# Another order for a hand-scheduled conv and max-pool kernel: weight blocks copied ahead of the casts, one more block turned before the first product

## The chip, the cores and the metric

The kernel runs on one core of one Trainium2 chip. The metric is the device time of one execution in microseconds (us), lower is better; runs are compared by their median. Engines are named as in the profile: PE is TensorE, DVE is VectorE, ACT is ScalarE, POOL is GpSimd, SP is SyncE, which issues DMAs.

## The reference

The input `x` is 16 images of 64 channels and 64 x 64 pixels, `weight` is 128 filters of 64 x 3 x 3, all float32. The reference is a 3 x 3 convolution with zero padding of one pixel, followed by a 2 x 2 maximum:

```python
conv[b, co] += weight[co, ci, kh, kw] * x_pad[b, ci, kh:kh+h, kw:kw+w]
...
output[b, c, i, j] = np.max(conv[b, c, 2*i:2*i+2, 2*j:2*j+2])
```

The output is 16 x 128 x 32 x 32 in float32.

## The kernel before, in words

**Tiling.** Two images lie on the 128 partitions, 64 channels each; a pair p of images has its own bf16 tile `xb[p]` of 66 rows (a zero row above and below). A step s takes 16 rows of a pair (one of four quarters, `PLACES`), which give eight output rows for each of the two images, h = 0 and 1. There are 32 steps; the last is cut into two halves, 31 and 32. Each image's product uses only 64 rows of PE's array, so the two images run side by side: PE works in two lanes, and `product` (L252) issues a matmul of one lane, then one of the other. One product is three matmuls (the three columns of the filter, L206) of up to 512 columns, into one of the eight PSUM banks.

**The computation.** A pooled row is the maximum of two convolution rows that share input rows, so the kernel works with differences and sums of input rows and of filter rows. For steps of kind W (`TYPES`, L37) it forms e (`row_e`), s (`row_sum`) and d (`row_d`) from `xb`, with `combine` (L300): a joint one covers two neighbouring quarters in one instruction of 1024 columns, a single one 512. Products P2 and P0 go to a bank ta, P3 and P1 to a bank tb; `seed` (SE) copies ta to tb, `evac` (EV) copies ta to SBUF, `rowmax` (MX) takes the maximum into tb on DVE, P1 adds the s product, `odd` (OD) copies the odd columns out on ACT, `colmax` (CM) takes the maximum with the even ones on DVE and sends the output when both images are done. With `+`, OD copies nothing and CM reduces directly. Steps of kind K use the rows of `xb` themselves: PA1, PA2 into ta, PB1, PB2 into tb, and PR adds the s product. Step 0 runs in half pieces, F.k.part: F.0 and F.1 go to ta, F.2 and F.3 to tb (`first_product`, L267).

**The weights.** The filter arrives as `wraw` in float32 (DMA at L81). g0, g1 and g2 are its three filter rows, cast to bf16 blocks of `wq` (`raw_block`, L166). D2 is g2 - g1, D0 is g0 - g1, GS is g0 + g2, GM and GP are GS - g1 and GS + g1 (L412 to L415). PE turns a block by three or four 128 x 128 transposes into a PSUM bank (TG0, TD2 and so on: `turn`, L142), and DVE or ACT copies it to `wt` (VG0, VD2 and so on: `turn_out`, L152). The ring blocks G1, GM and GP need one column block copied first (uG1, uGM, uGP: `ring`, L128), on ACT with a `+`, else on POOL. F.0 needs VD2, F.1 VG0, F.2 VD0 and F.3 VG2; PR and PRA need VG1, P2 needs VGM, P1 needs VGP. Eight matmuls on constants (L506) stand ahead of all turns.

**The rows.** Of pair 0, 49 rows come in float32 by SP's queue: `kfirst` in two pieces (L95), `ksecond` (L97) and `kthird` (L99). They are cast to `xb[0]` by XOa, XEa (odd and even rows of the first piece of kfirst), XOb, XEb (second piece), X1, X2 (ksecond), X3 and X4 (kthird). F.0 and F.1 read the XO rows, F.2 and F.3 the XE rows. The last 15 rows of pair 0 (L.0.49.64) and all other pairs (L.p.lo.hi, `load`, L327) come by POOL's queue, which casts on the way.

**What sets the order.** Nothing is scheduled by a tool: `ORDER` (L444) is a list of tokens written out, and each engine gets its instructions in that order. `BANKS` (L498) gives, in order of need, the PSUM bank of each turn, ta and tb. An engine waits for the data and for its bank to be free. POOL's instructions and loads also wait for the DVE operation on rows or weights that stands last ahead of them in the list (`on_gpsimd`, L70), and the first load waits for D2. A `+` moves a token to its other engine: EV, SE, D on DVE instead of ACT or POOL; E on POOL instead of DVE; XO, XE on ACT instead of DVE; `&` makes S and E joint. The V copies go to ACT for G0, G2 and GM and to DVE for D2, D0, G1 and GP, and a `+` exchanges that (L155); a g is cast on ACT, or on DVE with a `+`.

Closing access: for s = 32 `colmax` reads the two banks ta and tb of the image in one instruction,

```python
in_=acc[:, a : b + 1 : b - a, i0:i1].rearrange("p k r (w two) -> p r w k two", two=2)
```

Of the kernel before, what the change touches and what calls it, by code (L numbers as in the profile page):

```python
# [11 lines left out]
def kernel(  # L12
# [424 lines left out]
    for m in ("G0", "G1", "G2"):  # L437
# [17 lines left out]
        PB1.5.1 S.10 P3.6.1 P2.7.0 PA2.9.0 CM.2.1 MX.6.0 MX.6.1 P1.6.0 PB2.5.1 P2.7.1 D.10 OD.4.0 SE.7.0
        EV.9.0 MX.5.1 OD.6.0 P1.6.1 P0.7.0 P3.7.0 PR.5.1 P2.8.1 SE.7.1 EV.7.0 CM.4.0 CM.6.0 OD+.6.1 D.8 P2.8.0
        P0.7.1 CM.6.1 P3.7.1 PB1.9.0 MX.7.0 OD.5.1 CM.5.1 P1.7.0 SE.8.0 SE.8.1 E&.10 S.11 D+.11 P0.8.1 EV.7.1
        PB2.9.0 E&+.12 P0.8.0 OD.7.0 P3.8.0 EV.8.1 P2.10.1 P2.2.0 MX.7.1 EV.8.0 L.5.0.64 MX.9.0 PR.9.0 P3.8.1
        CM.7.0 MX.8.0 P1.8.0 P1.7.1 SE.10.1 P0.10.1 OD.7.1 P3.10.1 SE.2.0 P0.2.0 EV.10.1 MX.8.1 P2.11.0 CM.7.1
        P3.2.0 S&.12 P1.8.1 P2.10.0 MX.10.1 OD.8.0 OD.9.0 PA1.9.1 P1.10.1 CM.8.0 CM.9.0 D.14 PA1.15.1 OD.8.1  # L460
        EV.2.0 CM.8.1 SE.11.0 OD.10.1 SE.10.0 MX.2.0 PA2.9.1 P0.11.0 P1.2.0 CM.10.1 P0.10.0 P3.10.0 PB1.9.1
        P3.11.0 EV.11.0 PA1.15.0 EV.9.1 OD.2.0 P2.12.1 EV.10.0 D+.12 SE.12.1 S&.14 PA2.15.1 PB2.9.1 D+.13
        S&.17 MX.10.0 CM.2.0 MX.11.0 MX.9.1 D.19 L.6.0.64 P1.10.0 P0.12.1 PA2.15.0 EV.15.1 P2.11.1 P3.12.1
        EV.12.1 E+.14 OD.10.0 CM.10.0 SE.11.1 P1.11.0 EV.15.0 PR.9.1 P2.12.0 OD.11.0 P0.11.1 MX.12.1 CM.11.0
        P1.12.1 P2.13.0 OD.9.1 CM.9.1 D+.16 E&.20 S&.18 SE.12.0 EV.11.1 P0.12.0 E&.18 P2.14.1 P3.12.0 E&+.16
        SE.13.0 EV.12.0 P0.13.0 P3.11.1 SE.14.1 OD.12.1 D.17 P2.13.1 EV.13.0 SE.13.1 CM.12.1 P0.14.1 P3.13.0
        MX.12.0 P3.14.1 EV.14.1 MX.13.0 P2.14.0 P0.13.1 MX.11.1 SE.14.0 P1.12.0 P3.13.1 OD.12.0 P1.13.0
        MX.14.1 P0.14.0 P1.11.1 EV.13.1 P1.14.1 D.18 PB1.15.0 OD.13.0 CM.12.0 MX.13.1 CM.13.0 OD.11.1 PB1.15.1
        P3.14.0 D.21 PB2.15.0 P2.16.0 P2.17.1 CM.11.1 EV.14.0 OD.14.1 SE.17.1 CM.14.1 MX.14.0 MX.15.0 P1.14.0
        PR.15.0 P1.13.1 OD+.13.1 PB2.15.1 CM.13.1 SE.16.0 MX.15.1 P2.19.0 OD.14.0 P0.17.1 OD+.15.0 P3.17.1  # L470
        CM.15.0 PR.15.1 EV.17.1 MX.17.1 P0.16.0 P2.18.1 SE.19.0 CM.14.0 P3.16.0 OD.15.1 EV.16.0 P0.19.0
        P1.17.1 S&.21 MX.16.0 CM.15.1 P2.16.1 SE.18.1 OD.17.1 EV.19.0 P3.19.0 CM.17.1 MX.19.0 P0.18.1 SE.16.1
        P1.16.0 OD+.16.0 P2.18.0 P1.19.0 P3.18.1 EV.18.1 P2.17.0 P0.16.1 P3.16.1 SE.18.0 MX.18.1 EV.16.1
        OD.19.0 D.20 L.7.0.64 E&.22 P1.18.1 P2.21.1 P0.18.0 SE.17.0 CM.16.0 MX.16.1 OD.18.1 EV.18.0 P3.18.0
# [85 lines left out]
```

## Time and profile before

| what | us |
|---|---|
| median of 3 runs (103.0 to 103.2) | 103.07 |
| the profiled execution | 103.78 |
| its span, first to last instruction | 102.0 |
| PE busy | 95.7 |
| DVE busy | 91.2 |
| ACT busy | 82.3 |
| POOL busy | 56.7 |

The profile is of one execution. "Span" runs from the first to the last instruction of the program; the execution's own time is 1.78 us longer. A row of the timeline gives start, duration, engine, line of the kernel, operation, what is written and read, shape and count, and in brackets the idle time of the engine before it and what ended it. A row of the windows gives the stretch, its length, then for PE, PEld (PE's weight loads), DVE, ACT and POOL the busy time and the number of instructions, then the granted clock of PE, the share of the DMA engines and GB/s. The durations of matmuls overlap, so their starts are what to read.

### The profile page before, as it was taken

The numbers are of one execution on the slowest core, as the hardware profiler recorded it, in microseconds if no ns is written. First come the engines' busy times: TensorE is split into PE (matmuls) and PEld (weight loads), VectorE is DVE, ScalarE is ACT, GpSimd is POOL, SyncE is SP. The second block draws the span as 40 slices with busy tenths as digits, with TensorE's granted clock in tenths as the row PEclk, the third lists the DMA queues.
The fourth block names the chain that finished last, engine by engine and source line by source line (L and its number), as shares of the span: only waits on it lengthen the run. The fifth ranks groups of instructions, "written<-read, shape, count | busy, mean of one in ns | idle before, by whom it ended". The sixth has DMA issues, their size and how long they took to land.

```text
span 102.0 us, 2471 instructions
## 1 busy us (share of the span) xinstructions
PE 95.7 (94%) x897; PEld 59.5 (58%) x897; DVE 91.2 (89%) x199; ACT 82.3 (81%) x182; POOL 56.7 (56%) x43
## 2 busy tenths in 40 slices
...
GB/s 75 263 322 175 162 171 214 225 235 231 228 218 245 327 202 191 240 209 212 143 330 151 116 146 190 202 284 105 70 231 14 16 195 107 103 103 0 135 202 86
DMA packets 11293, 18.04 MB, mean 177 GB/s; under 512 B 784, under 2 KB 9360, under 8 KB 10640
## 3 DMA queue, kind: packets, MB, share of 16 engines
...
q10 hardware_dynamic: 272, 0.13, 0.4%
q8 instruction: 7, 0.11, 0.4%
...
## 4 chain that ended last, share of the span: by engine, by line
PE 88%; DMA 5%; DVE 1%; ACT 1%; SPq 0%; issue 0%; DVEq 0%
PE acc L197 88%; DMA kfirst<-in_x_dram 5%; DVE o L378 1%; PE acc L146 1%; ACT wt L162 0%; ACT xb L401 0%; SPq L81 0%; DVEq L555 0%
## 5 line engine op out<-in xcount | busy, mean ns | idle before, releaser
L197 PEld LDWEIGHTS <-wt 64*128 64x128 bf16 x864 | 56.2, 94 | 33.1 <-issue 4.2
L197 PE MATMUL acc<-d,wt 64*128 64x504 bf16 (+3 forms) x312 | 63.4, 373 | 0.0
L322 POOL TENSOR_TENSOR d<-xb 128x1024 bf16<-128x1024 bf16 x18 | 38.1, 2129 | 17.1 <-DVE s L308 9.0
L197 PE MATMUL acc<-s,wt 64*128 64x504 bf16 (+3 forms) x204 | 47.2, 367 | 0.0
L360 DVE TENSOR_TENSOR acc<-acc,ev 128x512 f32<-128x512 f32 (+1 forms) x64 | 42.1, 683 | 1.8 <-ACT od L370 0.4
L197 PE MATMUL acc<-e,wt 64*128 64x512 bf16 (+2 forms) x156 | 38.2, 372 | 0.0
L355 ACT COPY acc<-acc 128x512 f32<-128x512 f32 (+1 forms) x52 | 29.6, 576 | 3.5 <-PE acc L197 2.3
L349 ACT ACTIVATE ev<-acc 128x512 f32<-128x512 f32 (+1 forms) x51 | 29.9, 595 | 2.0 <-PE acc L197 1.3
L197 PE MATMUL acc<-xb,wt 64*128 64x504 bf16 (+6 forms) x192 | 27.2, 333 | 0.5 <-ACT wt L162 0.5
L370 ACT COPY od<-acc 128x256 f32<-128x256 f32 (+1 forms) x51 | 18.6, 374 | 5.2 <-PE acc L197 3.1
L389 DVE TENSOR_TENSOR o<-acc,od 128x256 f32<-128x256 f32 (+1 forms) x51 | 20.2, 410 | 0.9 <-ACT od L370 0.6
L308 POOL TENSOR_TENSOR e<-xb 128x512 bf16<-128x512 bf16 (+1 forms) x8 | 12.2, 1523 | 5.3 <-PE acc L197 2.7
L328 POOL DMA_DIRECT2D xb<-in_x_dram x11 | 6.2, 564 | 10.5 <-DVE xb L403 6.7
L308 DVE TENSOR_TENSOR s<-xb 128x1024 bf16<-128x1024 bf16 (+1 forms) x20 | 11.4, 575 | 0.2 <-ACT xb L401 0.2
L385 DVE TENSOR_REDUCE o<-acc 128x256 f32<-128x512 f32 x13 | 8.9, 682 | 0.2 <-PE acc L197 0.2
L345 ACT COPY ev<-acc 128x512 f32<-128x512 f32 x11 | 6.4, 588 | 0.9 <-PE acc L197 0.6
L308 DVE TENSOR_TENSOR e<-xb 128x1024 bf16<-128x1024 bf16 (+1 forms) x8 | 5.2, 649 | 0.0
L322 DVE TENSOR_TENSOR d<-xb 128x1024 bf16<-128x1024 bf16 (+1 forms) x8 | 5.2, 647 | 0.0
L506 PE MATMUL acc<-const-bfloat16-1.0 128*128 128x512 bf16 x8 | 3.6, 628 | 0.8 <-PEq L541 0.8
L146 PEld LDWEIGHTS <-wq 128*128 128x128 bf16 x25 | 2.2, 132 | 1.7 <-issue 0.8
L146 PE MATMUL acc<-ident,wq 128*128 128x128 bf16 x25 | 2.9, 291 | 0.0
L506 PEld LDWEIGHTS <-const-bfloat16-1.0 128*128 128x128 bf16 x8 | 1.0, 139 | 2.4 <-issue 2.4
(29 smaller groups left out, 18.0 us busy)
## 6 DMA issues: line engine op xcount, KB each, us to landing
...
xb<-in_x_dram POOLq DMA_DIRECT2D x5, 1024.0 KB, 11.4
...
xb<-in_x_dram POOLq DMA_DIRECT2D x1, 528.0 KB, 11.1
ksecond<-in_x_dram SPq DMA_DIRECT2D x1, 512.0 KB, 6.4
kthird<-in_x_dram SPq DMA_DIRECT2D x1, 512.0 KB, 7.1
...
```

What stands on the lines that cost most here:

```text
L146: nc.tensor.transpose(tp[:, (j - lo) * CO : (j - lo + 1) * CO], wq[:, j : j + 2, :].rearrange("a b c -> a (b c)"), ident,)
L197: nc.tensor.matmul(acc[:, t, i0:i1, o0:o1], wt[lo : lo + CI, tap_of(m0, kw, h), :], rows(lo, i0, i1, c0, c1), start=start and kw == 1, sto ...
L308: note(engine.tensor_tensor(out=dst, in0=in0, in1=in1, op=op))
L322: engine.tensor_tensor(out=row["d", s][:, 0:n, :], in0=t[:, f + 1 : f + 1 + n, :], in1=t[:, f - 1 : f - 1 + n, :], op=SUB)
L328: inst = on_gpsimd(nc.gpsimd.dma_start(out=xb[p][:, lo + 1 : hi + 1, :], in_=rows_of(p, lo, hi)))
L345: (nc.vector.tensor_copy if alt else nc.scalar.copy)(out=dst, in_=src)
L349: nc.scalar.mul(dst, src, -1.0)
L355: (nc.vector.tensor_copy if alt else nc.scalar.copy)(out=acc[:, t, i0:i1], in_=acc[:, ta[s, h], i0:i1])
L360: nc.vector.tensor_tensor(out=t, in0=t, in1=ev[s][:, h, i0:i1], op=MAX)
L370: nc.scalar.copy(out=dst, in_=acc[:, tb[s, h], i0:i1, 1::2])
L385: nc.vector.tensor_reduce(out=o[:, h, i0:i1], in_=t.rearrange("p r (w two) -> p r w two", two=2), axis=mybir.AxisListType.X, op=MAX)
L389: nc.vector.tensor_tensor(out=o[:, h, i0:i1], in0=t[:, :, 0::2], in1=od[s][:, h, i0:i1], op=MAX)
```

## The change

Only `ORDER` and `BANKS` differ; no function is touched. The tokens of the products are the same ones, in another order.

- Up to the first product, F.0.0, the old list turns five blocks (G2, D2, G1, D0, G0: 19 transposes), the new one six (D2, G0, D0, G1, G2, GP: 22). GM is turned later in both. The change was described in a few words as two more blocks turned ahead of the first product; by the list it is one, GP.
- Casts of the weights: D2 is first on DVE, g2 moves from DVE to ACT, GP comes fourth on DVE, and uGP moves from ACT to POOL.
- Copies out: VG0 moves from DVE to ACT, ahead of XOa; VD2 from ACT to DVE; VG2 from ACT to DVE; VGP from ACT to DVE. XEa moves from DVE to ACT, so that all four casts of kfirst are there, XOa, XEa, XOb, XEb, with uGM before the last.
- Loads: L.0.49.64 is the first on POOL's queue instead of the third; L.1.0.17 follows GM instead of XEa.
- Row operations: d on DVE eleven times instead of eight; e on DVE joint three times and single twice instead of seven and one, on POOL joint six times and single six times instead of three and five; s joint 15 times and single twice instead of 12 and 8; OD with `+` twelve times instead of thirteen.
- The end: the last pair of products is P1.31.0 with PRB.32.1 instead of PA2.32.0 with P1.31.1, and CM.31.1, CM.32.0, CM.32.1, CM.31.0 close, where it was CM.32.1, CM.32.0, CM.31.1.

The diff, cut to its beginning, two lines of the middle and its end:

```diff
     ORDER = """
-        g2+ g1 D2 g0 TG2 TD2 uG1+ XOa+ TG1 VD2+ VG2 D0 XOb+ GS+ XEa XEb+ X2 TD0 L.1.0.17 TG0 VD0 L.1.17.33
-        VG0+ F.0.0 GP uGP+ F.2.0 F.0.1 F.3.1 GM F.1.0 S.0 X1+ F.1.1 EV+.0.1 EV.0.0 F.3.0 F.2.1 VG1+ uGM+
-        PA1.1.0 PB1.1.0 L.0.49.64 PA2.1.0 MX.0.1 MX.0.0 PB2.1.0 PA1.1.1 PB1.1.1 PR.0.0 X4 PR.0.1 X3 L.1.33.64
-        L.2.0.33 S.1 L.2.33.64 OD+.0.1 PA2.1.1 CM.0.1 EV.1.0 PB2.1.1 S.3 PB1.3.1 PA1.3.0 PB1.3.0 MX.1.0
-        PA1.3.1 EV.1.1 OD.0.0 L.3.0.64 PA2.3.0 TGM MX.1.1 PR.1.1 PR.1.0 CM.0.0 PB2.3.1 PA2.3.1 S.2 OD.1.1
-        PB2.3.0 D+.2 E&.2 CM.1.1 VGM EV.3.0 OD+.1.0 TGP P2.4.1 PA1.5.0 CM.1.0 MX.3.0 PA1.5.1 PB1.5.0 EV.3.1
-        PA2.5.1 PA2.5.0 PR.3.0 SE.4.1 MX.3.1 D.4 VGP+ P0.4.1 PB2.5.0 P2.2.1 S.4 P3.4.1 EV.5.0 P2.4.0 PR.3.1
-        S.5 E&.6 S&.7 EV.5.1 EV.4.1 OD.3.0 P2.6.0 SE.2.1 MX.5.0 L.4.0.64 CM.3.0 PR.5.0 SE.4.0 P0.2.1 P3.2.1
-        OD.3.1 P0.4.0 P3.4.0 MX.4.1 EV.2.1 D.6 OD+.5.0 EV.4.0 CM.3.1 P2.6.1 PA1.9.0 SE.6.0 SE.6.1 CM.5.0 E+.8
...
-        P0.29.1 P2.31.0 P3.29.1 CM.28.1 SE.30.0 EV.30.1 EV.29.1 P0.30.0 D+.31 S&.30 P3.30.0 P2.31.1 MX.28.0
-        EV.30.0 SE.31.0 MX.30.1 MX.29.1 P1.28.0 P1.30.1 MX.30.0 P0.31.0 SE.31.1 OD.28.0 P0.31.1 P3.31.1
-        CM.28.0 P3.31.0 P1.29.1 EV.31.0 P1.30.0 MX.31.0 PB1.32.0 PA1.32.1 EV.31.1 OD.30.1 CM.30.1 PB1.32.1
-        P1.31.0 PRA.32.1 PA1.32.0 PB2.32.0 OD.30.0 PRB.32.0 MX.31.1 OD.31.0 OD.29.1 PRB.32.1 CM.30.0 PB2.32.1
-        CM.31.0 PA2.32.1 PRA.32.0 CM.29.1 P1.31.1 PA2.32.0 CM.32.1 CM.32.0 OD.31.1 CM.31.1
+        D2 g0 TD2 g2 GS+ D0 GP g1 TG0 uG1+ VG0 VD2 TD0 TG1 TG2 XOa+ uGP L.0.49.64 VD0 TGP XEa+ XOb+ VG2+ GM
+        uGM+ F.0.0 XEb+ F.2.0 L.1.0.17 F.1.0 L.1.17.33 F.0.1 F.1.1 F.2.1 X2 EV.0.1 X1+ L.1.33.64 EV+.0.0 F.3.0
+        F.3.1 X3 X4 PA1.1.1 PB1.1.1 MX.0.0 VGP PA2.1.1 S.0 PB2.1.1 PA1.1.0 PB1.1.0 PA2.1.0 PA1.3.1 PB1.3.1 S.1
+        L.2.0.33 PB2.1.0 VG1+ L.2.33.64 MX.0.1 EV.1.0 EV.1.1 MX.1.0 PR.0.0 PA1.3.0 PA2.3.1 OD.0.0 S&.5 PR.1.0
+        OD.1.0 PA2.3.0 CM.0.0 TGM PB2.3.1 MX.1.1 PR.1.1 PA1.5.0 PB1.3.0 EV.3.1 PA2.5.0 VGM PB1.5.0 PR.0.1
+        PA1.5.1 EV.3.0 OD.1.1 L.3.0.64 CM.1.0 E+.2 MX.3.1 D+.2 PB2.3.0 PR.3.1 OD.0.1 EV.5.0 PB2.5.0 PA2.5.1
+        S&.4 OD.3.1 P2.2.1 E.4 CM.1.1 EV.5.1 CM.0.1 SE.2.1 CM.3.1 MX.3.0 P2.4.0 PR.3.0 P2.4.1 P0.2.1 MX.5.0
+        D.4 S&.7 E&.6 D+.6 SE.4.1 P0.4.1 PR.5.0 SE.4.0 OD.3.0 CM.3.0 OD.5.0 P3.4.1 E+.8 EV.4.1 L.4.0.64 P3.4.0
+        P3.2.1 CM.5.0 P2.6.1 EV.2.1 P0.4.0 MX.4.1 EV.4.0 P1.4.1 P2.6.0 SE.6.0 PA1.9.0 SE.6.1 MX.2.1 P1.2.1
+        P0.6.0 D+.7 OD.4.1 OD.2.1 PA2.9.0 EV.6.0 S&.11 D+.10 CM.2.1 D.8 P3.6.0 L.5.0.64 MX.4.0 P2.7.0 P0.6.1
+        P3.6.1 EV.6.1 EV.9.0 P1.4.0 MX.6.0 P1.6.0 PB1.5.1 SE.7.0 PB2.5.1 OD.4.0 MX.6.1 P2.8.1 P1.6.1 CM.4.1
+        MX.5.1 OD.6.0 PR.5.1 P3.7.0 SE.8.1 P0.8.1 P0.7.0 P2.7.1 OD.6.1 CM.4.0 CM.6.0 P2.8.0 CM.6.1 EV.7.0
...
+        P2.21.1 OD+.18.1 SE.21.1 CM.18.1 MX.18.0 D+.22 P1.16.1 P3.17.0 P1.18.0 EV.17.0 OD.16.1 P2.22.0 P2.19.1
+        P3.19.1 SE.22.0 EV.19.1 SE.20.0 D.20 P1.21.1 P0.22.0 OD+.17.0 CM.17.0 D.23 MX.19.1 P2.22.1 P3.22.0
...
+        SE.29.1 P0.30.0 OD.28.1 P3.30.0 EV.30.0 MX.28.0 P1.28.0 P2.31.0 P0.29.1 CM.28.1 MX.30.0 SE.31.1
+        P1.30.0 P3.29.1 EV.29.1 OD+.28.0 MX.29.1 P0.31.1 SE.31.0 P0.31.0 P1.30.1 P3.31.0 CM.28.0 EV.31.1
+        PB1.32.0 OD.30.0 CM.30.0 OD.30.1 PA1.32.0 PRB.32.0 P3.31.1 P1.29.1 MX.31.1 PA1.32.1 EV.31.0 PRA.32.0
+        PB1.32.1 P1.31.1 OD.29.1 CM.30.1 PB2.32.0 PB2.32.1 CM.29.1 OD.31.1 MX.31.0 PA2.32.0 PRA.32.1 PA2.32.1
+        CM.31.1 CM.32.0 P1.31.0 PRB.32.1 CM.32.1 OD.31.0 CM.31.0
     """
     BANKS = (
-        "0123456710346520137365417346027351426507431270652347105234651370451275302641057631256401723451670312"
-        "745632071634025674123706153427601526314"
+        "0123456701246753240546307124156371053246713041507632140362051376042375106245273165473026145076342561"
+        "047531205634072514675012643572041574325"
     )
```

More of the change, by code (lines that the diff above doesn't have):

```diff
@@ L455 @@
[L455 to L474, printed above, removed]
@@ new lines @@
+        P3.2.1 CM.5.0 P2.6.1 EV.2.1 P0.4.0 MX.4.1 EV.4.0 P1.4.1 P2.6.0 SE.6.0 PA1.9.0 SE.6.1 MX.2.1 P1.2.1
+        P0.6.0 D+.7 OD.4.1 OD.2.1 PA2.9.0 EV.6.0 S&.11 D+.10 CM.2.1 D.8 P3.6.0 L.5.0.64 MX.4.0 P2.7.0 P0.6.1
+        P3.6.1 EV.6.1 EV.9.0 P1.4.0 MX.6.0 P1.6.0 PB1.5.1 SE.7.0 PB2.5.1 OD.4.0 MX.6.1 P2.8.1 P1.6.1 CM.4.1
+        MX.5.1 OD.6.0 PR.5.1 P3.7.0 SE.8.1 P0.8.1 P0.7.0 P2.7.1 OD.6.1 CM.4.0 CM.6.0 P2.8.0 CM.6.1 EV.7.0
+        SE.8.0 E&+.11 P3.8.1 PB1.9.0 EV.8.1 OD+.5.1 SE.7.1 CM.5.1 S&.12 S&.8 P0.8.0 P2.10.1 PB2.9.0 MX.7.0
@@ new lines @@
+        P3.8.0 P0.7.1 MX.9.0 EV.8.0 P1.7.0 PR.9.0 SE.10.1 EV.7.1 P3.7.1 P0.10.1 D.11 OD.7.0 MX.8.0 MX.7.1
+        CM.7.0 EV.10.1 P3.10.1 P2.2.0 D.14 MX.8.1 MX.10.1 SE.2.0 OD.9.0 P1.7.1 P1.8.0 P2.11.0 CM.9.0 P1.8.1
+        OD.8.0 OD.7.1 OD.8.1 P1.10.1 P0.2.0 SE.11.0 P3.2.0 CM.8.0 E&+.12 CM.7.1 CM.8.1 EV.2.0 OD+.10.1 CM.10.1
+        PA1.9.1 PA1.15.1 MX.2.0 PB1.9.1 PA2.15.1 PA2.9.1 P0.11.0 EV.11.0 P2.10.0 P1.2.0 SE.10.0 EV.15.1 D+.12
+        PB2.9.1 PA1.15.0 EV.9.1 P0.10.0 OD.2.0 E.16 P2.11.1 PA2.15.0 S&.15 S&.19 D+.16 MX.9.1 EV.10.0 P2.12.1
```

45 lines of the change are left out of this document (27 added, 18 removed).

## The prediction

> **What bounds the kernel now.** I read the page first: the busy shares, then its chain of work.
>
> ```profile
> span 102.0 us, 2471 instructions
> PE 95.7 (94%) x897; PEld 59.5 (58%) x897; DVE 91.2 (89%) x199; ACT 82.3 (81%) x182; POOL 56.7 (56%) x43
> PE 88%; DMA 5%; DVE 1%; ACT 1%; SPq 0%; issue 0%; DVEq 0%
> ```
>
> TensorE (PE) carries the end for 88% of the span. The chain in order of time says where it does not:
>
> ```profile
> 6.87 7.39 PE acc L197 x90
> ...
> 16.86 80.13 PE acc L197 x749
> 96.99 0.02 issue
> 97.01 1.29 DVE o L378 x2
> ```
>
> The first rows land at 5.9 (the ACT row at 5.92 below waits for them), ScalarE (ACT) casts them and copies a weight block, products run from 6.87 to 96.99, then VectorE (DVE) closes. So three things move the end: the start of the products, what lies among them, and the tail. For waits among them I read the windows; the count behind PE's busy time is matmuls.
>
> ```profile
> 20.00:30.00 10.00, 10.00 (x94) 5.88 (x92) 9.49 (x19) 9.07 (x21) 7.42 (x5) 1.00 1.06 229
> 30.00:40.00 10.00, 10.00 (x95) 6.15 (x92) 10.00 (x21) 9.27 (x21) 5.36 (x4) 1.00 1.01 245
> 40.00:50.00 10.00, 10.00 (x92) 5.04 (x90) 9.80 (x19) 9.35 (x21) 6.37 (x5) 1.00 0.96 201
> 50.00:60.00 10.00, 10.00 (x96) 6.88 (x94) 9.53 (x20) 8.44 (x19) 8.47 (x5) 1.00 0.61 196
> 60.00:70.00 10.00, 10.00 (x93) 6.71 (x90) 9.44 (x19) 9.64 (x23) 6.62 (x4) 1.00 0.82 185
> 70.00:80.00 10.00, 10.00 (x91) 5.58 (x88) 9.80 (x18) 9.25 (x21) 7.25 (x4) 1.00 0.30 106
> 80.00:90.00 10.00, 10.00 (x96) 7.26 (x93) 9.67 (x20) 8.97 (x22) 8.28 (x5) 1.00 0.31 107
> ```
>
> The fullest stages hold 96 matmuls; against them the seven lack 2, 1, 4, 0, 3, 5, 0, together 15. PE runs two lanes with .22 from matmul to matmul in each (rows below), so each is worth .11: about 1.6 us of waits that the busy share hides. DVE (third busy figure) stands at 94 to 100%, nearly a second bound.
>
> **The change, part by part.** The products and their number stay; order, engines and banks move. All times are us.
>
> *The start.* The rows that the new order reshuffles:
>
> ```profile
> 3.63 0.98 ACT L172 CAST wq<-wraw 128x192 bf16<-128x192 f32 x2 [1.61 <-DMA wraw<-in_weight_dram]
> 4.51 0.24 ACT L132 COPY wq<-wq 128x64 bf16<-128x64 bf16 x1
> 4.19 2.21 PE L146 MATMUL acc<-ident,wq 128*128 128x128 bf16 x19
> 4.88 0.48 DVE L176 TENSOR_TENSOR gsum<-wraw 128x192 f32<-128x192 f32 x1
> 5.92 0.41 ACT L401 CAST xb<-kfirst 128x256 bf16<-128x256 f32 x1 [1.17 <-DMA kfirst<-in_x_dram]
> 6.23 1.07 ACT L162 COPY wt<-acc 128x512 bf16<-128x512 bf16 x2
> 7.19 0.42 ACT L401 CAST xb<-kfirst 128x256 bf16<-128x256 f32 x1
> 7.20 0.49 PE L197 MATMUL acc<-xb,wt 64*128 64x256 bf16 x6
> 7.66 0.28 PE L197 MATMUL acc<-xb,wt 64*128 64x256 bf16 x2
> ```
>
> ACT now runs g0, g2, g1, uG1, VG0, XOa, XEa, XOb, uGM, XEb. The casts start .44 apart (.98 for two of .54), so g1 ends at 5.05 and uG1 (.24) near 5.3. VG0 needs TG0: turns start .107 apart (19 in 2.21, the last .31 long), TD2 and TG0 are eight, the last ends at 5.25. VG0 runs from 5.30 and lets the next start .48 later (two copies in 1.07, the second .59), at 5.78; so XOa still starts with its rows, at 5.92, and ends at 6.33. DVE has VD2 done near 5.7. What decides is PE's queue: 22 turns instead of 19 stand ahead of F.0.0. From 4.19 the last starts at 6.44 and a product follows .15 later (below), at 6.60, when XOa is done. F.0.0 starts at 6.60 instead of 6.87: **-.27**.
>
> TGP needs uGP, which moves from ACT to POOL, behind GP (DVE's fourth weight operation, where GS was, so done near 5.4). No row shows such a copy. Its 64 columns lie below POOL's 128-column select (.29) and far below a 512-column e there:
>
> ```profile
> 1.02 0.29 POOL masks.py:199 TENSOR_SCALAR_AFFINE_SELECT ident<-ident 128x128 bf16<-128x128 bf16 x1
> 89.08 1.15 POOL L308 TENSOR_TENSOR e<-xb 128x512 bf16<-128x512 bf16 x1
> ```
>
> I take .3, done by 5.8, .4 before TGP's turn. At 1.15 TGP would start at 6.7 and every product behind it: +.11 instead of -.27.
>
> F.2.0 started at 7.20; its three pairs take .33 (F.0.0's did, 6.87 to 7.20), so F.0.1 was due at 7.53 and started at 7.66, when XOb had ended on ACT (7.61) behind two weight copies. In the new order XEa (about .46, a row more than .42) and XOb directly follow XOa; XOb ends near 7.0, F.0.1 is due at 7.50: **-.13**.
>
> What else moved between ACT and DVE has its cover: VD0 ends by 6.2 and VG2 by 6.9, ahead of F.2.0 (due 6.93) and F.3.0 (8.48). XEb waits on ACT behind uGM, that for GM (7.3), and ends at 7.9, ahead of F.2.1 (8.16); without GM's .25 of cover it would hold PE. The covers shrink behind it: X1 (second rows at 8.5) ends at 9.0 for PA1.1, due 9.14; EV.0.0 frees bank 6 at 9.6 for PB1.1, due 9.79. Second rows .2 later would already be felt.
>
> The terms hold if the first rows land as late as in this execution. The runs' median is 103.07, the profiled execution took 103.78 (its span and 1.78 around it), .71 more. With rows landing at 5.2, the old order could start at 6.25 (last turn from 6.11) without waiting for XOb: 6.87 + .13 - 6.25 = .75 sooner, which would explain the .71. The new order couldn't follow: its 22 turns end at the same time, 6.60, a start term of **+.35**. The landing row says late, the two times say early; I take the middle of -.40 and +.35, **-.02**, and keep both ends.
>
> The Trainium skill (TensorE: Matmul & The Clock Gate, Part 1) gives the array half rate until a free-running window of some 3.4 us has been busy. This trace agrees: turns .107 apart before 6.4, under .07 at 16.5. By that rule a window that ends after the new start runs its first products at half pace and takes back up to half of the .27, an estimated .13.
>
> *TGP among the products.*
>
> ```profile
> 14.69 0.38 PE L197 MATMUL acc<-xb,wt 64*128 64x504 bf16 x1
> 14.91 0.38 PE L197 MATMUL acc<-xb,wt 64*128 64x504 bf16 x1
> 16.20 0.38 PE L197 MATMUL acc<-xb,wt 64*128 64x504 bf16 x2
> 16.52 0.34 PE L146 MATMUL acc<-ident,wq 128*128 128x128 bf16 x3
> 16.79 0.39 PE L197 MATMUL acc<-xb,wt 64*128 64x512 bf16 x1
> ```
>
> After 16.20 a matmul was due .22 later, at 16.42; it came at 16.79: **-.37** once TGP is gone from here. (Three turns .06 apart and .15 to the product make 16.52 to 16.79.) TGM stays. By the order's text one block more, not two, is turned ahead of the first product, so this is earned once. The ends are 0 (if the slot was idle anyway) and -.37.
>
> *The tail.*
>
> ```profile
> 97.74 0.27 ACT L370 COPY od<-acc 128x128 f32<-128x128 f32 x1 [1.84 <-DVE o L378]
> 98.22 0.28 DVE L389 TENSOR_TENSOR o<-acc,od 128x128 f32<-128x128 f32 x1
> ```
>
> PE ends at 96.99. Both closing reductions (.69 each, the second .61 after the first: 1.29 - .68) wait for it: CM.32.1 reads banks 1 and 3, an access that spans bank 2, where the last product P1.31.1 writes. CM.31.1 then ends at 98.50. In the new order CM.32.0 spans banks 2 to 4, and the last pair (P1.31.0, PRB.32.1) writes 7 and 5, so it may start one pair (.33) before the end, at 96.68 on the old scale; CM.32.1 at 97.29, CM.31.0 at 97.89 to 98.17: **-.33**. It hides behind the last pair; if CM.31.1 ahead of it on DVE is late, the gain falls to 0.
>
> *The middle.* DVE gets three d's more, and of the e's three joint and two single instead of seven and one, of the s's 15 and 2 instead of 12 and 8.
>
> ```profile
> L322 POOL TENSOR_TENSOR d<-xb 128x1024 bf16<-128x1024 bf16 x18 | 38.1, 2129 | 17.1 <-DVE s L308 9.0
> L322 DVE TENSOR_TENSOR d<-xb 128x1024 bf16<-128x1024 bf16 (+1 forms) x8 | 5.2, 647 | 0.0
> L308 DVE TENSOR_TENSOR s<-xb 128x1024 bf16<-128x1024 bf16 (+1 forms) x20 | 11.4, 575 | 0.2 <-ACT xb L401 0.2
> ```
>
> On DVE that is .65 for 1024 columns and, from the last row, (11.4 - 12 x .65) / 8 = .45 for 512. So +1.95, -2.15, -.75: DVE loses about 1 us of 91. So I see no reason for more waits, nor a sure one for fewer: **0**, between -1.6 (all gone) and +1.6 (doubled). L.0.49.64 goes first there and pair 1's rows come one load later; S&.4 and E.4, planned at 17, need them, about .9 before P2.4 at 18.6.
>
> Sum: -.02 - .37 - .33 + 0 = -.72; 103.07 - .72 = 102.35, say **102.4**. Late rows alone give 102.0, early rows 102.7.
>
> **Rivals.**
>
> *The third rows come late (slower).*
>
> ```profile
> 2.60 0.43 SPq L99 DMA_DIRECT2D kthird<-in_x_dram  x1
> kthird<-in_x_dram SPq DMA_DIRECT2D x1, 512.0 KB, 7.1
> 10.19 1.14 ACT L401 CAST xb<-kthird 128x512 bf16<-128x512 f32 x2
> 12.00:15.00 3.00, 3.00 (x31) 1.42 (x29) 3.00 (x7) 1.23 (x3) 0.88 (x2) 1.00 1.06 159
> ```
>
> kthird lands at 9.7 and ACT took it at 10.19. Now L.0.49.64 (240 KB) issues at about 5.8 (before, the first load waited for a cast, to 6.6), while SP's rows still stream. If its packets go between, at 159 GB/s they hold kthird up by 1.5, to 11.2: X3, X4 (.52 apart), then VG1 on ACT to about 12.9, and PR.0.0, due at 11.73, starts 1.2 late. It decides from a landing after 10.1; it gives 102.4 + 1.2 = 103.6. Against it: most of kthird should be through before that load's packets begin (the old first load issued at 6.6, and kthird still landed in time). The Trainium skill (DMA: Bandwidth & Descriptors, Queues, rings and completion order) states round robin between queues by packet, which speaks for it.
>
> *DVE is the real bound (no change).* Then an earlier start of PE only lengthens its waits. For it: DVE at 94 to 100%. Against: the chain never passes through DVE before 97. Near 103.0.
>
> *The middle waits more (slower).* D.20 on POOL now queues behind D+.22 on DVE, a 2.1 us operation with .9 to spare before P0.20.0; joint e's on POOL have gone from three to six. If the waits double: 104.0.
>
> *The middle waits vanish.* 102.4 - 1.6 = 100.8; halved, 101.6.
>
> *It doesn't do what it says:* if uGP is slow on POOL, TGP is turned ahead but holds all products; the .38 above, 102.7.
>
> **How the numbers follow.** Forecast .48 (101.9 to 102.8, by the rows' landing), fewer waits .08, slow uGP .04, DVE bound .12, third rows .12, more waits .16. A measurement of this kernel can tell about 0.2%, .21. Faster: the first three, less .02 that may fall inside that: **.58**. Same: DVE bound and those .02, **.14**. Slower: the other two, **.28**. Range **101.6 to 103.9**: it leaves out the far part of fewer waits and of more waits, and takes in all else.
>
> **What would show it.** F.0.0 at 6.60 (6.55 to 6.65) straight behind three turns; no wait before F.0.1; TGM alone among the products; a closing reduction that starts before PE's end; about 15 matmuls missing from 20 to 90; X3 starting before 10.1. Wrong if F.0.0 comes after 6.9, if PE stands before PA1.1 or PR.0.0, or if the stages lack 20 matmuls or more.

## The result and the profile after

The changed kernel takes 101.7 us (median of 4 runs, 101.4 to 102.1), the kernel before 103.13 beside it (103.0 to 103.25); the ratio is 0.9864, 95% interval 0.9823 to 0.9905. Forecast was 102.4: the sign was right and the time lies in the range, but the gain, 1.4, is twice the forecast .72. For one kernel below, the old order with exchanged row pieces, the ratio is that of three executions out of seven; the other four took 2 us longer, and the text there says why.

The page of the changed kernel, its first line, the busy shares and the chain's shares:

```profile
span 99.7 us, 2479 instructions
PE 94.7 (95%) x897; PEld 58.6 (59%) x897; DVE 90.6 (91%) x196; ACT 83.6 (84%) x182; POOL 57.2 (57%) x45
...
PE 95%; DVE 1%; DVEq 1%; issue 0%
```

The busy shares hardly moved. The chain in order of time (start, duration, what) tells more:

```profile
4.35 2.17 PE acc L146 x22
6.52 7.19 PE acc L197 x90
13.71 0.27 PE acc L146 x3
13.98 81.14 PE acc L197 x762
...
95.15 0.69 DVE o L378
95.84 0.60 DVEq L555
96.44 0.20 DVE o L389
```

DMA has gone from it (5% before): the products now follow 22 turns directly. One group of three turns (TGM) interrupts the products instead of two. The beginning in the timeline, POOL's copy for uGP, ACT and PE:

```profile
5.36 0.24 POOL L134 COPY wq<-wq 128x64 bf16<-128x64 bf16 x1 [4.05 <-DVE wq L415]
5.24 0.59 ACT L162 COPY wt<-acc 128x512 bf16<-128x512 bf16 x1
5.74 1.07 ACT L401 CAST xb<-kfirst 128x256 bf16<-128x256 f32 x3
7.26 0.24 ACT L132 COPY wq<-wq 128x64 bf16<-128x64 bf16 x1 [0.45 <-DVE wq L414]
9.26 1.14 ACT L401 CAST xb<-kthird 128x512 bf16<-128x512 f32 x2 [0.16 <-DMA kthird<-in_x_dram]
5.64 0.88 PE L146 MATMUL acc<-ident,wq 128*128 128x128 bf16 x8
6.45 0.61 PE L197 MATMUL acc<-xb,wt 64*128 64x256 bf16 x8
```

The first cast starts at 5.74, right behind VG0 and with the rows just landed (5.72); two more follow without a gap, and F.0.0 starts at 6.45 behind the turns. XOb, the third, is done at 6.81, and F.0.1 starts at 7.37 without a wait; X3 starts at 9.26. The stages, columns as before:

```profile
20.00:30.00 10.00, 10.00 (x93) 5.28 (x93) 10.00 (x21) 9.13 (x21) 6.46 (x5) 1.00 1.06 234
30.00:40.00 10.00, 10.00 (x95) 5.79 (x95) 10.00 (x20) 8.76 (x20) 6.30 (x3) 1.00 1.02 260
40.00:50.00 10.00, 10.00 (x96) 5.62 (x92) 10.00 (x20) 9.72 (x23) 6.83 (x6) 1.00 0.81 193
50.00:60.00 10.00, 10.00 (x97) 7.69 (x95) 9.98 (x20) 8.88 (x20) 7.66 (x5) 1.00 1.03 256
60.00:70.00 10.00, 10.00 (x96) 6.87 (x93) 9.78 (x20) 9.64 (x21) 8.45 (x5) 1.00 0.37 130
70.00:80.00 10.00, 10.00 (x95) 6.51 (x93) 9.85 (x21) 9.53 (x22) 6.98 (x4) 1.00 0.25 90
80.00:90.00 10.00, 10.00 (x96) 6.12 (x93) 9.80 (x18) 9.68 (x22) 6.49 (x4) 1.00 0.37 127
```

Against 96 they lack 3, 1, 0, -1, 0, 1, 0: four matmuls, where it was 15. DVE is even fuller than before (9.78 to 10.00 against 9.44 to 10.00) and yet products wait less. At the end, the last four matmuls, DVE and ACT:

```profile
94.94 0.50 PE L197 MATMUL acc<-s,wt 64*128 64x252 bf16 x4
95.15 1.29 DVE L378 TENSOR_REDUCE o<-acc 128x128 f32<-128x512 f32 x2 [0.32 <-PE acc L197]
95.38 0.27 ACT L370 COPY od<-acc 128x128 f32<-128x128 f32 x1 [0.87 <-PE acc L197]
96.36 0.28 DVE L389 TENSOR_TENSOR o<-acc,od 128x128 f32<-128x128 f32 x1
```

The first closing reduction starts at 95.15, beside the last matmul of a product, which starts at 95.17. The two profiled executions, cut at the same events (starts of the first and the last matmul of a product, DVE's last end, the execution's own time):

| part | before | after | difference | forecast |
|---|---|---|---|---|
| start of F.0.0 | 6.87 | 6.45 | -.42 | -.27 with late rows |
| first to last product | 89.84 | 88.72 | -1.12 | -.13 (XOb) - .37 (TGP) |
| last product to DVE's end | 1.79 | 1.47 | -.32 | -.33 |
| DVE's end to the execution's end | 5.28 | 4.86 | -.42 | 0 |
| sum | 103.78 | 101.50 | -2.28 | |

The last part is not chance, though neither the start, the middle nor the tail makes it. In the seven profiled executions of kernels with 43 instructions on POOL (x43 in the page's busy line: the kernel before, and all that was made from it but for one) it is 5.26 to 5.38. In the six with 44 or 45 (the new head in the old order, the changed kernel and most of what was made from that; all are described below) it is 4.86 to 4.99. The difference lies in POOL's closing instructions on semaphores, behind all work. Their first and last start, before and after:

```profile
L555 POOLq EVENT_SEMAPHORE  x4: 17/17/17, 100.9 to 101.9; - x4
...
L555 POOLq EVENT_SEMAPHORE  x4: 17/17/17, 99.0 to 99.6; - x4
```

In the kernel before, the second of them starts .44 behind the first (100.86, 101.30), after the change .09. The delay stands ahead of the 69th POOL instruction of the trace, all kinds counted, in all seven, and also in the one kernel with 41, where it comes later in the closing sequence (5.22 in all). So nearly all of this .42 goes with the number of instructions on POOL; no run changed that number alone.

Of the 1.12, .50 is accounted for by XOb and TGP; **.62 is left, from the middle**, where the forecast had 0.

### The profile page after: what moved, and what is told of

It reads as the page before. It is cut to its first block, busy times and chain, and to the rows that moved or that the text cites. A ratio compares the mean times of both kernels' runs of the same rounds, so it can differ in the third digit from the quotient of the medians.

```text
span 99.7 us, 2479 instructions
## 1 busy us (share of the span) xinstructions
PE 94.7 (95%) x897; PEld 58.6 (59%) x897; DVE 90.6 (91%) x196; ACT 83.6 (84%) x182; POOL 57.2 (57%) x45
## 4 chain that ended last, share of the span: by engine, by line
PE 95%; DVE 1%; DVEq 1%; issue 0%
PE acc L197 89%; PE acc L506 4%; PE acc L146 2%; DVE o L378 1%; DVEq L555 1%; DVE o L389 0%
## 5 line engine op out<-in xcount | busy, mean ns | idle before, releaser
L197 PEld LDWEIGHTS <-wt 64*128 64x128 bf16 x864 | 55.2, 94 | 33.0 <-issue 2.7
L197 PE MATMUL acc<-s,wt 64*128 64x504 bf16 (+2 forms) x204 | 47.7, 367 | 0.0
L360 DVE TENSOR_TENSOR acc<-acc,ev 128x512 f32<-128x512 f32 (+1 forms) x64 | 42.9, 683 | 1.8 <-PE acc L197 1.1
L322 POOL TENSOR_TENSOR d<-xb 128x1024 bf16<-128x1024 bf16 (+1 forms) x15 | 30.8, 2064 | 12.0 <-DVE d L322 6.0
L197 PE MATMUL acc<-xb,wt 64*128 64x504 bf16 (+6 forms) x192 | 26.0, 333 | 0.0
L308 POOL TENSOR_TENSOR e<-xb 128x512 bf16<-128x512 bf16 (+1 forms) x12 | 19.6, 1642 | 8.3 <-PE acc L197 4.1
L385 DVE TENSOR_REDUCE o<-acc 128x256 f32<-128x512 f32 x12 | 8.2, 679 | 0.0
L322 DVE TENSOR_TENSOR d<-xb 128x1024 bf16<-128x1024 bf16 x11 | 7.5, 683 | 0.0
L308 DVE TENSOR_TENSOR e<-xb 128x1024 bf16<-128x1024 bf16 (+1 forms) x5 | 3.1, 620 | 0.0
L172 ACT CAST wq<-wraw 128x192 bf16<-128x192 f32 x3 | 1.4, 536 | 1.5 <-DMA wraw<-in_weight_dram 1.5
```

Of the source, the lines that this page charges most:

```text
L197: nc.tensor.matmul(acc[:, t, i0:i1, o0:o1], wt[lo : lo + CI, tap_of(m0, kw, h), :], rows(lo, i0, i1, c0, c1), start=start and kw == 1, sto ...
L308: note(engine.tensor_tensor(out=dst, in0=in0, in1=in1, op=op))
L322: engine.tensor_tensor(out=row["d", s][:, 0:n, :], in0=t[:, f + 1 : f + 1 + n, :], in1=t[:, f - 1 : f - 1 + n, :], op=SUB)
L360: nc.vector.tensor_tensor(out=t, in0=t, in1=ev[s][:, h, i0:i1], op=MAX)
L385: nc.vector.tensor_reduce(out=o[:, h, i0:i1], in_=t.rearrange("p r (w two) -> p r w two", two=2), axis=mybir.AxisListType.X, op=MAX)
```

## The experiments

Times are medians; ratios are to the kernel before on the same chip.

### The old order again, the new head in the old order

The first kernel is a copy of the kernel before. The second has the new start and nothing else of the change; TGP stays among the products:

```diff
-        g2+ g1 D2 g0 TG2 TD2 uG1+ XOa+ TG1 VD2+ VG2 D0 XOb+ GS+ XEa XEb+ X2 TD0 L.1.0.17 TG0 VD0 L.1.17.33
-        VG0+ F.0.0 GP uGP+ F.2.0 F.0.1 ...
+        D2 g0 TD2 g2 GS+ D0 GP g1 TG0 uG1+ VG0 VD2 TD0 TG1 TG2 XOa+ uGP L.1.0.17 VD0 XEa+ XOb+ VG2+ L.1.17.33
+        F.0.0 XEb+ F.2.0 X2 F.0.1 ...
```

> The kernel before, a second time, for a second profile. Theory A (the first rows land late in every execution, at 5.7 to 5.9 us): F.0.0 at 6.8 to 6.9 us again, F.0.1 waiting .1 us for XOb, and the profiled execution's span within .4 us of 102.0. Theory B (the rows land early in the timed runs, which is why their median was .7 us under the profiled execution): rows by 5.2 us, F.0.0 near 6.3 us, span near 101.3 us.

> The kernel before with the new order's head up to the first product (copies out ahead of the casts, uGP on POOL early), but TGP left where it was. Theory A (each term of the sum adds up): 19 turns end near 6.0 us and XOa near 6.15 us, so F.0.0 starts at 6.2 us instead of 6.87, F.0.1 does not wait; the rest is as before, so 103.1 - .65 - .13 = 102.3 us. Rival (DVE and the loads set the middle, an earlier start only lengthens the waits there): F.0.0 equally early, but 102.8 to 103.1 us, with more matmuls missing from 20 to 90 us.

The copy: 103.3, ratio 0.9991 (0.9966 to 1.0016). Theory B holds: in its profiled execution the first rows landed at 4.34 instead of 5.9, F.0.0 started at 6.35 instead of 6.87, nothing waited for XOb, and behind that the waits of the middle came back at the same products with the same lengths: the wait of P2.21.1 was .25 at 60.99 and is .26 at 60.34. So the waits belong to the order and move along with its start.

The new head: 102.74, ratio 0.9939 (0.9915 to 0.9963). F.0.0 came at 6.15, but part of that was given back:

```profile
8.65 0.43 DVE L403 CAST xb<-ksecond 128x512 bf16<-128x512 f32 x1 [1.09 <-DMA ksecond<-in_x_dram]
...
9.13 0.61 PE L197 MATMUL acc<-xb,wt 64*128 64x512 bf16 x4 [0.22 <-DVE xb L403]
```

PA1.1 stood .40 for X1, whose rows landed at 8.62. An early start is worth nothing beyond what the second rows allow. Neither theory's account holds: against the copy's profiled execution F.0.0 came .20 sooner and the second rows took .40 back. What this kernel gains is about .3 that a later experiment (one instruction more) explains, and .39 behind DVE's end (4.87 against 5.26).

### TGP late, and the old end

Both start from the changed kernel: one turns TGP behind F.3.1 (with the list of banks to match), the other puts CM.32.0 behind CM.32.1.

```diff
-        ... L.0.49.64 VD0 TGP XEa+ XOb+ VG2+ GM uGM+ F.0.0 ... F.3.0 F.3.1 X3
+        ... L.0.49.64 VD0 XEa+ XOb+ VG2+ GM uGM+ F.0.0 ... F.3.0 F.3.1 TGP X3
```
```diff
-        CM.31.1 CM.32.0 P1.31.0 PRB.32.1 CM.32.1 OD.31.0 CM.31.0
+        CM.31.1 P1.31.0 PRB.32.1 CM.32.1 CM.32.0 OD.31.0 CM.31.0
```

> The changed kernel with TGP behind F.3.1 instead of ahead of F.0.0, same bank. Theory A: F.0.0 starts three slow turns (.25 to .32 us) sooner, TGP costs .37 us between products at 9 us: +.05 to +.12 us, 101.8 us, the same within the measurement. Rival (turning GP ahead is what pays, its place among products costs .37 us and more while the start can't come sooner because of the rows): +.35 to +.5 us, 102.1 us.

> The changed kernel with CM.32.0 behind CM.32.1 in DVE's order, so that both closing reductions stand behind the last product as before. Theory A: +.3 us, 102.0 us, CM.31.0 about 1.5 us behind PE's last matmul start plus .3. Rival (the last output's landing on the other queue hides it): 0, 101.7 us.

TGP late: 102.16, ratio 0.988 (0.9849 to 0.991), the rival's time. In the trace it takes 2.96 instead of 2.56 from F.0.0 to the first matmul behind the 48 of step 0, so the three turns cost .40 there, the forecast .37; .26 more comes at 22 to 26 behind loads that landed about 1.1 later. F.0.0 came at 6.20 instead of 6.45, which gives part of this back. The time's interval overlaps that of the changed kernel. The old end: 101.72, ratio 0.9858 (0.9815 to 0.9901); from the last product's start to DVE's end it takes 1.79, as before the change, against 1.47. The .32 stands on the trace alone: the medians, 101.72 and 101.70, don't show it. The last output doesn't hide it, since what lies behind DVE's end is the same (4.87 and 4.86); in the profiled execution an F.0.0 .27 sooner (6.18) makes up for it, and single executions scatter by .4 and more.

### Two waits removed by hand, in the old order

```diff
-        ... OD.19.0 D.20 L.7.0.64 E&.22 P1.18.1 P2.21.1 P0.18.0 SE.17.0 CM.16.0 MX.16.1 OD.18.1 ...
+        ... OD.19.0 D.20 L.7.0.64 P1.18.1 P2.21.1 P0.18.0 SE.17.0 CM.16.0 MX.16.1 E&.22 OD.18.1 ...
-        ... CM.22.0 OD+.20.0 E&+.26 SE.23.0 OD.22.1 CM.20.0 MX.20.1 ...
+        ... MX.20.1 CM.22.0 OD+.20.0 E&+.26 SE.23.0 OD.22.1 CM.20.0 ...
```

> The kernel before with two tokens moved and nothing else: the joint e of steps 22 and 23 on DVE goes behind MX.16.1 (it stood right ahead of CM.16.0, for whose bank P2.21.1 waited .25 at 61), and MX.20.1 goes ahead of CM.22.0 and CM.20.0 (P1.20.1 waited .24 for it at 72.3). Theory (each wait of the middle belongs to one DVE or ACT operation that stands too late in the list): both waits go, none grows behind them, the stream from the first to the last product takes 89.2 to 89.4 instead of 89.7 to 89.84, and the time falls by .4 to .5, ratio about 0.996. Rival (DVE is nearly the bound, so what is won comes back as longer waits a little later): the two waits go, others grow by as much, and the time is that of the kernel before, ratio 1.000.

Measured: 104.81, ratio 1.0145 (1.0109 to 1.0182). Both theories missed: it is 1.5 slower, and each move has its own reason. P2.21.1 no longer waits. But D.22 on POOL stands behind the e that was moved, so it runs later, and meets the next s on DVE. The rows of POOL and DVE in this kernel:

```profile
61.27 2.12 POOL L322 TENSOR_TENSOR d<-xb 128x1024 bf16<-128x1024 bf16 x1 [2.21 <-DVE e L308]
62.30 1.65 DVE L308 TENSOR_TENSOR s<-xb 128x1024 bf16<-128x1024 bf16 x1
```

and the same s in the kernel before:

```profile
62.72 0.68 DVE L308 TENSOR_TENSOR s<-xb 128x1024 bf16<-128x1024 bf16 x1
```

1.65 instead of .68: the s ends .55 behind the end of POOL's d (63.39), as if it had run only then. CM.16.1 and P2.20.0 behind it start late (a wait of .60). The Trainium skill (SBUF — State Buffer, Who interferes with whom) says that a DVE instruction with two SBUF inputs contends with a GpSimd instruction that reads SBUF, and calls the contention an exclusive lock; this trace agrees. In the trace of the kernel before three such pairs overlap, by .13, .06 and .01, and none is slowed: POOL's operations stand right behind a row operation of DVE, and DVE has PSUM operations beside them. The changed kernel has longer ones, the two longest of .29 and .32, and there an s took .85 and an e .88.

The second move put MX.20.1 ahead of CM.22.0, which frees bank 4 for SE.23.0. CM.22.0 ended at 72.32, SE.23.0 started at 72.43 after 1.24 of idle, and P0.23.0 waited .81. A third piece, .37 at 45 to 47, isn't due to the moves: E&.20 waited .39 for the rows of pair 5, whose last DMA engine was done at 45.00 in this execution (43.33 in the profiled one of the kernel before).

### More and less work for DVE

```diff
-        E&+.19 ... E&+.21 ... E&+.27 ... E&+.28
+        E&.19 ... E&.21 ... E&.27 ... E&.28
```

This one is the changed kernel. The other two leave work out: the chosen joint e's compute one half, which both steps read (steps 10, 18, 20, 22 of the old order; 6, 22, 24 of the new one).

```diff
     def row_e(s, alt, joint):
+        if s in (10, 18, 20, 22):
+            combine("e", e_pool, SUB, s, False, alt)
+            row["e", neighbour(s)] = row["e", s]
+            return
         combine("e", e_pool, SUB, s, joint, alt)
```

> The changed kernel with four joint e's (steps 19, 21, 27, 28 and their neighbours) back on DVE from POOL, at their places in the list: seven joint ones there, as in the kernel before, 2.7 us more of DVE. Theory (the new order waits less because row operations left DVE's queue ahead of the CM and MX that products wait for): waits come back in the stages from 40 to 90, some .3 to .7 in all, and the time rises by as much, to 102.0 to 102.4, ratio to the kernel before 0.990 to 0.994. Rival (the places of single tokens matter, not how much work DVE has): at most one of the four stands ahead of an operation that a product waits for, the stream stays at 88.7 to 88.9, and the time at 101.7, ratio 0.985.

> The kernel before, where four joint e's on DVE (tokens of steps 10, 18, 20 and 22) compute 512 columns instead of 1024 and the neighbouring step reads the same half: work is left out, about 1.0 us of DVE (4 x .26), no token moves. Theory (DVE is a second bound in the middle, so each us of its work has a price; four joint e's added to the changed kernel, 2.7 us, lengthened its stream by 2.3): the 1.0 us less shorten the stream by .5 to .9, from 89.7 to 88.8 to 89.2, ratio 0.991 to 0.995; this is about what the new order saves of DVE's work and of the stream's length. Rival (only the places of single operations matter): the stream gets shorter by the .25 of the wait behind the e of step 22 at most, ratio 0.998 to 1.000.

> The changed kernel with the same omission in its three joint e's on DVE (steps 6, 22, 24): .8 us less of DVE. Theory (the price falls as the waits run out; only about .6 us of waits is left in the middle of the changed kernel, half of it on ScalarE's operations): the stream gets shorter by .1 to .3, from 88.72 to 88.4 to 88.6, ratio to the kernel before 0.982 to 0.986. Rival (DVE still sets the pace there): shorter by .5 or more, ratio 0.981 or less.

Four e's back on DVE: 104.02, ratio 1.0078 (1.0048 to 1.0108), more than the theory's most. 2.3 more of DVE's busy time (92.9 against 90.6) lengthen the stream (from the first product's start to the last's) from 88.72 to 91.11. The profiled execution ended 2.41 later: its start came .34 sooner, and .36 more lies behind DVE's end, at the place on POOL named above. The page's busy line and two stages:

```profile
PE 95.7 (94%) x897; PEld 55.3 (54%) x897; DVE 92.9 (91%) x200; ACT 83.4 (82%) x182; POOL 48.8 (48%) x41
```
```profile
50.00:60.00 10.00, 9.96 (x90) 6.14 (x86) 10.00 (x20) 8.20 (x19) 4.60 (x3) 1.00 1.02 261
...
80.00:90.00 10.00, 9.92 (x91) 6.25 (x92) 9.75 (x20) 9.18 (x20) 5.71 (x4) 1.00 0.27 93
```

The stages lack 7, 1, 2, 6, 6, 8, 5 matmuls (in the first, DVE also waited for rows in this execution). P1.18.1, for one, waits .43 for MX.18.1, right behind an e of .68 at 58.84.

Half e's in the old order: 102.85, ratio 0.9962 (0.9937 to 0.9987). 1.0 us less of DVE did not bring the .5 to .9 of the theory: from the 192nd product matmul on, the stream takes 70.57 instead of 70.81, and .22 of this .24 lies at the wait behind the e of step 22. Before and after the omission, one stage with that wait and one without:

```profile
40.00:50.00 10.00, 10.00 (x92) 5.20 (x90) 9.26 (x20) 9.28 (x22) 7.76 (x6) 1.00 0.95 212
...
60.00:70.00 10.00, 10.00 (x96) 6.43 (x93) 9.43 (x20) 9.52 (x22) 7.08 (x5) 1.00 0.78 198
```

60 to 70 holds 96 matmuls instead of 93; 40 to 50 stays at 92, though DVE lost work there too (9.26 busy instead of 9.80). So a us of DVE's work has no fixed price: taken away, it was worth the waits that stand right behind it; added, it pushes every MX and CM behind it until DVE's next idle time, of which there is little, and here cost about its own length.

Half e's in the new order: 101.66, ratio 0.9855 (0.9813 to 0.9897), no gain that can be told from the changed kernel. Its profiled execution is the slowest of six and shows why these times scatter:

```profile
24.48 0.69 DVE L308 TENSOR_TENSOR s<-xb 128x1024 bf16<-128x1024 bf16 x1 [0.77 <-DMA xb<-in_x_dram]
```

S&.11 needs the second half of pair 2, landed at 24.39 here and at 22.75 in the changed kernel; CM.2.1 stands behind it, and PB1.5.1 waited .97 for that. The prediction named such a risk for the rows of pair 1. Here it is pair 2: in the changed kernel the margin is .8 (22.75, and S&.11 at 23.58), and in this execution it was used up.

### One instruction more on DVE

```diff
+    nc.vector.memset(wq[:, GM, :], 0.0)
```

> The kernel before with one small memset more on DVE ahead of the weights, while it is idle. In the kernel before and three kernels made from it DVE starts MX.22.1 .41 after the semaphore event that it waits for, at one and the same instruction, and in the kernel with the new head it doesn't. Theory (the delay belongs to a place in DVE's instruction stream, not to data): with one instruction more the .44 of idle before MX.22.1 goes or moves to another instruction, and the .24 before P1.20.1 with it. Rival (it belongs to the data or the moment): it stays before MX.22.1. The time stays within the scatter.

One execution: 102.7. The timeline of DVE in the kernel before, where MX.22.1 is the row of line 360, and the same place with the memset (all lines one further down):

```profile
69.18 0.41 DVE L389 TENSOR_TENSOR o<-acc,od 128x256 f32<-128x256 f32 x1
70.04 0.70 DVE L360 TENSOR_TENSOR acc<-acc,ev 128x512 f32<-128x512 f32 x1 [0.45 <-ACT od L370]
```
```profile
68.39 0.41 DVE L390 TENSOR_TENSOR o<-acc,od 128x256 f32<-128x256 f32 x1
68.88 0.70 DVE L361 TENSOR_TENSOR acc<-acc,ev 128x512 f32<-128x512 f32 x1
```

The idle time falls from .45 to .08, P1.20.1 no longer waits, and from the 192nd product matmul on the stream takes 70.52 instead of 70.81. What MX.22.1 needs was there at 69.58 (P3.22.1's end) in the kernel before. So about **.3 of the old order's waits hang on the place of one instruction in DVE's stream**, not on the order of the work. The old order shows it in six profiled executions of kernels with DVE's original count; the new head and this memset are free of it, and the changed kernel has no idle time of this kind (its longest on DVE from 20 to 90 is .22). The trace has a hint of the cause. The page lists DMA queues as `instruction`; the packets of one of them, q14, are of 8 KB. In those six executions one of them starts .64 to 1.23 behind the late MX.22.1 (70.68 in the kernel before), and with the memset it starts at 68.62, ahead of MX.22.1. In the kernel before another starts at 101.90, .60 behind the late instruction of POOL at the end; after the change the one before the last comes at 85.98. So instructions seem to be supplied in blocks, and the step to the next block to cost about .4 where nothing covers it. That this is the cause isn't shown.

### Rows made late in both orders

```diff
-    for lo, hi in ((0, MID), (MID, FAR)):
+    for lo, hi in ((MID, FAR), (0, MID)):
```

> The kernel before with the two pieces of kfirst loaded in the opposite order, so that the piece that the first casts need lands second, at about 6.3 instead of 4.3 to 5.9. Theory (in the old order F.0.0 comes .95 to .97 behind the landing, since ScalarE copies a weight block between the cast and the product): F.0.0 at 7.2 to 7.4, the time .4 to .9 above the kernel before, 103.8 to 104.2, ratio about 1.006. Rival (a later start only takes away waits further on): the stream gets shorter by as much and the time stays, ratio 1.000.

> The changed kernel with the same exchange of the two pieces of kfirst. Theory (the weight blocks are copied out ahead of the casts, so F.0.0 follows the landing by one cast, .45, and not by .97): F.0.0 at 6.7 to 6.85 instead of 6.2 to 6.45, the time .3 to .5 above the changed kernel, 102.0 to 102.2, and the difference between the two orders grows from 1.4 to 1.8 or 1.9. Rival (both orders only follow the landing): F.0.0 as late as in the old order, the difference stays at 1.4 or less.

The old order: three executions took 104.0 to 104.7, ratio 1.0096 (1.0056 to 1.0136), and four took 106.0 to 106.4. The new order: 102.07, ratio 0.988 (0.9848 to 0.9912), all six between 101.5 and 102.3. So the orders lie 2.2 apart here, by the ratios, more than the 1.8 or 1.9 expected, since the old order lost 1.0 and not .4 to .9. The old order's cast, weight copies and first product, then its windows:

```profile
6.63 0.41 ACT L401 CAST xb<-kfirst 128x256 bf16<-128x256 f32 x1 [1.78 <-DMA kfirst<-in_x_dram]
6.95 1.07 ACT L162 COPY wt<-acc 128x512 bf16<-128x512 bf16 x2
7.58 0.39 PE L197 MATMUL acc<-xb,wt 64*128 64x256 bf16 x3 [1.84 <-ACT wt L162]
```
```profile
6.00:8.00 2.00, 0.42 (x8) 0.39 (x10) 1.37 (x5) 1.37 (x4) 0.69 (x1) 1.00 0.78 320
8.00:10.00 2.00, 2.00 (x24) 1.55 (x22) 1.24 (x4) 1.28 (x5) 0.82 (x3) 0.50 0.67 90
10.00:12.00 2.00, 2.00 (x26) 1.54 (x24) 0.69 (x1) 0.89 (x3) 1.30 (x3) 0.65 0.97 158
```

and the new order's:

```profile
6.34 1.07 ACT L401 CAST xb<-kfirst 128x256 bf16<-128x256 f32 x3 [0.41 <-DMA kfirst<-in_x_dram]
6.79 0.65 PE L197 MATMUL acc<-xb,wt 64*128 64x256 bf16 x8 [0.67 <-ACT xb L401]
```

From landing to F.0.0: .97 in the old order (6.61 to 7.58), .47 in the new one (6.32 to 6.79), both as expected. That is what the copies ahead of the casts do. The four long executions weren't expected: the granted clock (.50 in the second window) fell to half at 8.00, 3.41 behind its grant at 4.58, and came back 3.41 later; in the profiled one of them the first 48 product matmuls took 4.22 instead of 2.67. PE had idled for 1.84 before 7.58, from 5.74 on (not from 6.2, as the expectation below has it). The Trainium skill (TensorE: Matmul & The Clock Gate, Part 1) has the clock follow how busy the array was in free-running windows of about that length; the trace agrees, and adds that a window busy for 1.6 of its 3.4 (turns until 5.74, products from 7.58) was not enough.

```diff
+        if s == "VD0":
+            for _ in range(4):
+                nc.tensor.matmul(acc[:, 7]..., ones[:, 0:128], ones, start=True, ...)
```

> The kernel before with the pieces of kfirst exchanged (rows late), and four matmuls on constants, into a bank that nothing uses yet, between the last turn and F.0.0. Without them three executions took 104.0 to 104.7 and four 106.0 to 106.4; in the profiled one of the latter the granted clock fell to half from 8.00 to 11.41, one window of 3.41 behind its grant at 4.58, in which PE had stood idle from 6.2 to 7.58. Theory (PE's idle time before the first product costs it the clock of the next window, in the executions whose window lies so): with PE kept busy the clock stays and all executions take 104.0 to 104.7. Rival (another cause of the slow executions): about half of them still take 106.

104.35, ratio 1.0104 (1.0063 to 1.0146), six executions from 103.7 to 104.8, none at 106. The window in which the clock had fallen:

```profile
8.00:10.00 2.00, 2.00 (x38) 1.80 (x36) 1.48 (x4) 1.49 (x5) 1.05 (x3) 1.00 0.82 108
```

38 matmuls instead of 24. In this execution the rows also landed sooner (5.85 against 6.61, F.0.0 at 6.82), so the window alone proves little; what speaks for the theory is that none of six is long, where four of seven were. Four matmuls that compute nothing kept the clock, as far as six executions can tell.

## Why the prediction was right, and where a term was wrong

**The start** was priced by the middle of two cases, -.02, and both cases exist. With late rows: forecast F.0.0 6.87 to 6.60 and no wait for XOb, measured 6.87 to 6.45 and none. With early rows the forecast was 6.25 for the old order and 6.60 for the new one, +.35. Measured at like times of the clock's grant (3.4 to 6.4 by execution): old 6.35, 6.00, 5.93, 5.74; new 6.45, 6.31, 6.18, 6.11 (the first with rows at 5.72, but set by its turns); +.10 to +.37. The 6.60 was .15 too late: the turns began at 4.14 instead of 4.19, and I carried .107 per turn to the end, while the clock was granted at 6.20 in that execution and the last turns came .08 and .05 apart. So the granted clock shortened the turns themselves, and did not take anything back from the .27.

**TGP out of the stream**, -.37: right, .40 with TGP put back. "This is earned once" holds: TGM is still there at 13.64 in the trace.

**The tail**, -.33: right, .32 in the trace.

**The middle**, 0: the step that failed. It read: "DVE loses about 1 us of 91. So I see no reason for more waits, nor a sure one for fewer: 0, between -1.6 (all gone) and +1.6 (doubled)." Measured: -.62. The prediction took the 15 lacking matmuls as one count and did not ask what each wait hung on. About .3 is the idle time before MX.22.1, which hangs on an instruction's place and which the list of the change doesn't show. The rest, about .3, is order: single operations that stood right ahead of an MX or CM that a product waited for, the e of step 22 (.25) the clearest. The sum of DVE's work, on which I argued, doesn't give the gain: 1.0 us less brought .24. It does give the loss when work is added: 2.3 more cost 2.4. The .3 for the order is what is left by subtraction; that the same operations of the new order save it one by one isn't shown.

**Behind DVE's end** the sum had no term, so 0: the second step that failed. Measured: -.42, which goes with the number of instructions on POOL.

**Median against profile.** With early rows the measured terms give +.26 (mean of the four) - .37 - .62 - .32 - .42 = -1.47, with late rows the table's -2.28; the medians' difference is -1.43. Early rows are the rule: in nine of the eleven profiled executions with this order of loads the first piece landed at 4.3 to 4.7, and at 5.7 and 5.9 only in the first one of each kernel. So the prediction explained the .71 rightly by late rows (F.0.0 at 6.87 instead of 6.35, and .13 for XOb), and the middle of two cases was not needed: the medians most likely stand for the early case, for which the forecast was 102.7 (where the rows landed in the executions that were only timed, no row shows). That the time still lies in the range is in part luck: two terms put at nothing, -.62 and -.42, outweigh a start that came out at +.26 and not at -.02. The measured 101.7 is .1 inside the range, below the 101.9 to 102.8 of the forecast case.

**The rivals.** Late third rows: fell; L.0.49.64 went out at 5.53, kthird landed at 9.24, X3 started at 9.26. DVE the real bound: fell as it was put; the waits move with the start and don't grow. An earlier start was lost only ahead of PA1.1, where the second rows, not DVE, are the limit (.40); work added to DVE did lengthen the stream. More waits: fell, the count of lacking matmuls went from 15 to 4. Waits halved or gone ("100.8; halved, 101.6") is what came nearest; it had .08. A slow uGP: fell, .24 on POOL against .3 taken.

The experiments point to no version that beats the changed kernel: what they undo or move costs time or changes nothing that can be told.
